# A decoder layer in split float32r: every weight product 256 columns wide, three in a row on one PSUM region

## The chip, the cores and the metric

The kernel runs on one core of one Trainium2 chip. The metric is device time in microseconds; the figure shown for the kernel before is the median of three runs. The profile is one execution, whose span runs from the first to the last instruction.

## What is computed

One layer of a hybrid decoder on a residual stream h of 256 rows by 2048, all float32: a half-step SwiGLU feed-forward network (FFN 1), token mixing, cross-attention to 256 memory rows, and a second half-step FFN (FFN 2). Cut to what the change touches:

```python
def swiglu_ffn(x, w_gu, w_down):                 # w_gu 2048 x 11264, w_down 5632 x 2048
    gate, up = jnp.split(x @ w_gu, 2, axis=-1)
    return (jax.nn.silu(gate) * up) @ w_down
...
    f = swiglu_ffn(rms_norm(h, ffn1_pre_g[l]), ffn1_w_gu[l], ffn1_w_down[l])
    h = h + FFN_RES_SCALE * rms_norm(f, ffn1_post_g[l])
    z = rms_norm(h, mix_pre_g[l]) @ w_in[l]      # conv a and g, then q, k, v, 1024 columns each
...
    y = jnp.concatenate([conv_out, attn], axis=-1) @ w_out[l]
    h = h + rms_norm(y, mix_post_g[l])
    c = memory_cross_attention(...)              # 4 heads of 128
    h = h + rms_norm(c, xattn_post_g[l])
    f = swiglu_ffn(rms_norm(h, ffn2_pre_g[l]), ffn2_w_gu[l], ffn2_w_down[l])
```

The two FFNs hold most of the arithmetic. The convolution group has a depthwise convolution with 31 taps, which is worked off on VectorE and on ScalarE with GpSimd.

## The kernel before

**Three products for one.** Each float32 operand is split into two float32r parts: `hi`, a copy of it rounded by ScalarE, and `lo`, what is left of it after VectorE has subtracted `hi`. A product x w is then taken as x_hi w_hi + x_lo w_hi + x_hi w_lo, three matmuls that accumulate in PSUM. The rows of x lie transposed in chunks (`ck` in the profile), where `xk[:, 0, :]` is the high and `xk[:, 1, :]` the low part of the 256 tokens for one k, a block of 128 rows of the contraction; the two lie next to each other, so that `xk` is also an operand of 512 columns.

**Weights.** Class `Weights` lists all weight tiles (128 x 1024, 512 KB) in the order of their use. SyncE loads them into `raw` (4 buffers), ScalarE makes `hi` (4 buffers, lines 177 and 179), VectorE `lo` (3 buffers, lines 193 and 195). A few tiles that are used later than they are split are held in chunks. Between tiles, class `Background` issues other work: gates, norms, convolution taps, attention.

**Four ways of multiplying.**
- `proj_T` (lines 423 and 426): the weights are stationary, the rows move, 256 columns wide. For a k and its regions (a region is half a PSUM bank, 256 columns) it issues first the two products with `hi`, region after region, then all products with `lo`. It is used for the first two of the 22 groups of gate and up in each FFN, for the GLU of the convolution group, for q and k, for the memory's keys (`kv_k`) and for the queries of the cross-attention.
- `gate_up` for the other 20 groups (lines 637 and 639): the weights are stationary and `xk` moves as one operand of 512 columns, into four banks in turn, so that a bank's left half gets x_hi w_hi and its right half x_lo w_hi; then four products of `lo` with x_hi, 256 wide, go on top of the right halves. A group thus holds four banks, and each has two partial sums.
- `proj` (lines 434, 436, 438): the rows are stationary and the weights move, 512 columns wide, over one or two banks in turn. It is used by `down` (FFN down and the output projection), for v, and for the output of the cross-attention. In `down` the last three tiles of the second half are kept back and go region by region, nine products on one bank.
- The values of the cross-attention (`mm_xv`, lines 1078 to 1080): rows stationary, weights moving, 256 columns wide, the three products of one region in a row. The change leaves this one as it is.

**The gate.** `queue_gate` lays the work on a finished group into the background: `add_parts` copies the right halves out of PSUM on ScalarE and adds the left halves on VectorE (for the first two groups it only copies), then come the scale, the SiLU, the product of gate and up, and its split into `hi` and `lo`.

Of the kernel before, what the change touches and what calls it, by code (L numbers as in the profile page):

```python
# [14 lines left out]
P = 128  # L15
# [27 lines left out]
class Background:  # L43
    """Work that is issued a piece at a time between the weight tiles."""
# [13 lines left out]
    def urgent(self, pieces):  # L58
        """Each of the pieces in a step of its own, before all else that waits."""
        for fn, dve, act in reversed(pieces):  # L60
            self.main.appendleft(None)
            self.main.appendleft((fn, dve, act, 0.0))
# [33 lines left out]
class Weights:  # L96
    """The weights in the order of their use: loads, then the two float32r parts, ahead of the products."""
# [22 lines left out]
    def start(self):  # L120
        """The first rows and weights, in halves."""
# [24 lines left out]
    def parts(self, i, whole):  # L146
        """The pieces of an entry that have a gain each: (raw, part of the tile, gain)."""
# [76 lines left out]
def layer_kernel(ctx: ExitStack, tc: tile.TileContext, x, mem, eye, consts, smalls, post_g, xt, memt,  # L224
# [127 lines left out]
    class Rows:  # L352
        """Transposed float32r parts of [256, 2048] rows, and their 1 / rms."""
# [64 lines left out]
    def proj_T(regions, first, last, hi, lo, xk, parts_first=False):  # L418
        order = [(f, r) for f in range(2) for r in enumerate(regions)]
        if not parts_first:  # L420
            order = [(f, r) for r in enumerate(regions) for f in range(2)]
        for f, (j, (ps, o)) in order:
            nc.tensor.matmul(ps[:, o:o + 256], hi[:, j * P:(j + 1) * P], xk[:, f, :],  # L423
                             start=first and o == 0 and f == 0, stop=False, skip_group_check=True)
        for j, (ps, o) in enumerate(regions):
            nc.tensor.matmul(ps[:, o:o + 256], lo[:, j * P:(j + 1) * P], xk[:, 0, :],  # L426
                             start=False, stop=last, skip_group_check=True)

    def proj(pss, first, last, hi, lo, xk, t, n0=0):
        xh = xk[:, 0, t * P:(t + 1) * P]  # L430
        xl = xk[:, 1, t * P:(t + 1) * P]
        cols = [slice((n0 + n) * 512, (n0 + n + 1) * 512) for n in range(len(pss))]
        for ps, c in zip(pss, cols):
            nc.tensor.matmul(ps, xh, hi[:, c], start=first, stop=False)  # L434
        for ps, c in zip(pss, cols):
            nc.tensor.matmul(ps, xl, hi[:, c], start=False, stop=False)  # L436
        for ps, c in zip(pss, cols):
# [820 lines left out]
```

## Time and profile before

| | us |
|---|---|
| median of 3 runs (1978.13 to 1981.71) | 1979.76 |
| span of the profiled execution | 1979.2 |
| TensorE busy | 1925.5 (97%) |
| VectorE busy | 1268.0 (64%) |
| ScalarE busy | 1098.7 (56%) |
| GpSimd busy | 204.8 (10%) |

In the profile a matmul has two parts, the load of its stationary operand (LDWEIGHTS, listed as PEld) and the product itself (MATMUL, listed as PE); 11034 of each ran. Matmuls are pipelined, so that the durations of neighbours overlap, and how fast a stream goes is read from the distance between starts. FFN 1's gate and up run from the start to 500 us, its down phase to 745 us, token mixing to 1137 us, cross-attention to 1234 us, FFN 2's gate and up to 1724 us, its down phase to the end. The granted TensorE clock is 0.997 of 2.4 GHz over the span.

### The profile page before, as it was taken

What the parts mean: (1) busy time and instruction counts of PE and PEld (TensorE: products, weight loads), DVE (VectorE), ACT (ScalarE), POOL (GpSimd) and SP (SyncE); (2) the same over time, 40 slices, a digit from 0 to 9 for tenths busy, and PEclk for the clock granted to TensorE, in tenths of its full rate; (3) what the DMA queues carried; (4) which work ended last, traced back from release to release, by engine and by line L of the source; (5) the groups of instructions that cost most, each with busy time, mean ns of one, the idle gap of its engine ahead of it and who ended that gap; (6) DMA issues with size and microseconds to landing.
All of it is one profiled execution on the core that took longest, in us unless ns stands there. A gap on an engine that the chain in (4) does not pass through costs nothing.

```text
span 1979.2 us, 29214 instructions
## 1 busy us (share of the span) xinstructions
PE 1925.5 (97%) x11034; PEld 1675.8 (85%) x11034; DVE 1268.0 (64%) x1774; ACT 1098.7 (56%) x1793; POOL 204.8 (10%) x192
## 2 busy tenths in 40 slices
PE   8999999999999999887899999999999999999998
PEld 8888888888888889886797898988888888888886
DVE  5666666666544556999767576666666666644444
ACT  6655555555434646766465565755555555533433
POOL 0000000000000000768401000000000000000000
PEclk9999999999999999999999999999999999999999
DMA  8666666666655774344555653566666666666664
GB/s 289 187 190 191 191 192 190 189 189 192 210 191 187 256 244 141 130 149 139 166 165 169 214 179 120 181 191 191 188 189 191 191 191 192 212 188 187 189 189 142
DMA packets 102094, 369.62 MB, mean 187 GB/s; under 512 B 11456, under 2 KB 11712, under 8 KB 101184
## 3 DMA queue, kind: packets, MB, share of 16 engines
q1 hardware_dynamic: 100944, 361.00, 58.5%
q10 hardware_dynamic: 1008, 6.75, 0.9%
q8 instruction: 86, 1.41, 0.3%
q14 instruction: 56, 0.46, 0.1%
HBM read 365.61 MB, written 2.10 MB: 186 GB/s over the span
## 4 chain that ended last, share of the span: by engine, by line
PE 89%; DVE 6%; issue 2%; POOL 2%; ACT 1%; DMA 1%; SPq 0%; DVEq 0%; POOLq 0%; ACTq 0%
PE ps L637 30%; PE ps L639 15%; PE ps L438 11%; PE ps L434 10%; PE ps L436 10%; PE ps L423 7%; PE ps L426 3%; DVE lo L195 3%; DVE cv L747 2%; POOL cv L758 1%; PE ps L339 0%; DMA raw<-in_f_gu_dram 0%; ACT hi L179 0%; PE ps L1080 0%; PE ps L1078 0%
## 5 line engine op out<-in xcount | busy, mean ns | idle before, releaser
L195 DVE SCALAR_TENSOR_TENSOR lo<-raw,sm,hi 128x512 fp32r<-128x512 f32 (+1 forms) x830 | 636.4, 806 | 335.1 <-issue 249.3
L179 ACT ACTIVATE hi<-raw,sm 128x512 fp32r<-128x512 f32 (+1 forms) x830 | 576.4, 741 | 374.8 <-PE ps L637 220.9
L637 PE MATMUL ps<-ck,hi 128*128 128x512 f32 x2560 | 693.4, 393 | 0.0
L637 PEld LDWEIGHTS ps<-ck,hi 128*128 128x128 f32 x2560 | 434.5, 188 | 55.0
L193 DVE TENSOR_TENSOR lo<-raw,hi 128x1024 fp32r<-128x1024 f32 x216 | 265.4, 1230 | 282.4 <-PE ps L438 248.6
L639 PEld LDWEIGHTS ps<-ck,lo 128*128 128x128 f32 x2560 | 388.0, 188 | 53.8
L639 PE MATMUL ps<-ck,lo 128*128 128x256 f32 x2560 | 399.5, 278 | 0.0
L177 ACT ACTIVATE hi<-raw 128x1024 fp32r<-128x1024 f32 x216 | 228.7, 1060 | 297.2 <-PE ps L436 253.0
L438 PE MATMUL ps<-lo,ck 128*128 128x512 f32 x896 | 286.6, 397 | 9.1 <-DVE lo L195 7.8
L434 PE MATMUL ps<-hi,ck 128*128 128x512 f32 x896 | 286.7, 397 | 1.0 <-ACT ck L347 1.0
L436 PE MATMUL ps<-hi,ck 128*128 128x512 f32 x896 | 285.2, 396 | 0.0
L423 PE MATMUL ps<-ck,hi 128*128 128x256 f32 x1664 | 229.3, 283 | 9.5 <-ACT hi L140 6.2
L423 PEld LDWEIGHTS ps<-ck,hi 128*128 128x128 f32 x1664 | 210.2, 189 | 10.6 <-ACT hi L140 6.2
L438 PEld LDWEIGHTS ps<-lo,ck 128*128 128x128 f32 x896 | 168.1, 188 | 53.5 <-DVE lo L195 10.9
L436 PEld LDWEIGHTS ps<-hi,ck 128*128 128x128 f32 x896 | 168.3, 188 | 41.8 <-DVE ck L350 0.4
L434 PEld LDWEIGHTS ps<-hi,ck 128*128 128x128 f32 x896 | 168.0, 188 | 41.6 <-ACT ck L347 1.2
L606 POOL TENSOR_TENSOR tmp<-tmp,rb 128x512 f32<-128x512 f32 x44 | 58.2, 1322 | 1125.1 <-ACT tmp L605 1105.8
L426 PE MATMUL ps<-ck,lo 128*128 128x256 f32 x832 | 129.4, 283 | 23.3 <-DVE lo L195 23.3
L426 PEld LDWEIGHTS ps<-ck,lo 128*128 128x128 f32 x832 | 110.5, 188 | 28.3 <-DVE lo L195 28.2
L758 POOL TENSOR_TENSOR cv<-cv,cf 128x255 f32<-128x255 f32 (+14 forms) x120 | 106.3, 887 | 31.9 <-ACT cf L757 23.7
L747 DVE SCALAR_TENSOR_TENSOR cv<-yv,cf,cv 128x255 f32<-128x255 f32 (+14 forms) x120 | 85.1, 709 | 2.7
L598 DVE TENSOR_TENSOR tmp<-ps,tmp 128x256 f32<-128x256 f32 x160 | 60.1, 417 | 10.2 <-ACT tmp L597 10.2
(142 smaller groups left out, 925.8 us busy)
## 6 DMA issues: line engine op xcount, KB each, us to landing
raw<-in_f_gu_dram SPq DMA_DIRECT2D x351, 512.0 KB, 4.1
raw<-in_f_down_dram SPq DMA_DIRECT2D x176, 512.0 KB, 4.3
raw<-in_w_in_dram SPq DMA_DIRECT2D x80, 512.0 KB, 3.6
raw<-in_w_out_dram SPq DMA_DIRECT2D x32, 512.0 KB, 3.6
cf<-in_post_g_dram ACTq DMA_DIRECT2D x4, 1024.0 KB, 6.9
raw<-in_x_k_dram SPq DMA_DIRECT2D x8, 512.0 KB, 3.9
raw<-in_x_q_dram SPq DMA_DIRECT2D x8, 512.0 KB, 4.3
raw<-in_x_o_dram SPq DMA_DIRECT2D x8, 512.0 KB, 4.3
```

The source lines that it names most:

```text
L177: self.nc.scalar.activation(dst, src, AF.Copy)
L179: self.nc.scalar.activation(dst, src, AF.Copy, scale=g)
L193: self.nc.vector.tensor_tensor(dst, src, hi.bitcast(F32), ALU.subtract)
L195: self.nc.vector.scalar_tensor_tensor(dst, src, g, hi.bitcast(F32), ALU.mult, ALU.subtract)
L423: nc.tensor.matmul(ps[:, o:o + 256], hi[:, j * P:(j + 1) * P], xk[:, f, :], start=first and o == 0 and f == 0, stop=False, skip_group_chec ...
L426: nc.tensor.matmul(ps[:, o:o + 256], lo[:, j * P:(j + 1) * P], xk[:, 0, :], start=False, stop=last, skip_group_check=True)
L434: nc.tensor.matmul(ps, xh, hi[:, c], start=first, stop=False)
L436: nc.tensor.matmul(ps, xl, hi[:, c], start=False, stop=False)
L438: nc.tensor.matmul(ps, xh, lo[:, c], start=False, stop=last)
L637: nc.tensor.matmul(ps, hi[:, w], xk, start=k == 0, stop=False, skip_group_check=True)
L639: nc.tensor.matmul(ps[:, 256:512], lo[:, w], xk[:, 0, :], start=False, stop=k == KT - 1, skip_group_check=True)
L758: nc.gpsimd.tensor_tensor(cv[:, ct, s:], cv[:, ct, s:], pr[:, :S - s], ALU.add)
```

## The change

- `proj_T` issues for each region its three products in a row: `hi` with x_hi, `hi` with x_lo, `lo` with x_hi. Only the very first k of an FFN's first group keeps the three parts apart.
- `proj` takes each 512 columns in two halves of 256, and for each half the three products in a row.
- `gate_up` uses `proj_T` for all 22 groups, with two banks to a group. There are no partial sums any more, and `add_parts` is gone: the scale and the product of gate and up read PSUM themselves.

All weights, loads and splits stay, and so do the buffers. The comments and docstrings that the diff removes are left out here.

```diff
     def proj_T(regions, first, last, hi, lo, xk, parts_first=False):
-        order = [(f, r) for f in range(2) for r in enumerate(regions)]
-        if not parts_first:
-            order = [(f, r) for r in enumerate(regions) for f in range(2)]
-        for f, (j, (ps, o)) in order:
-            nc.tensor.matmul(ps[:, o:o + 256], hi[:, j * P:(j + 1) * P], xk[:, f, :],
-                             start=first and o == 0 and f == 0, stop=False, skip_group_check=True)
-        for j, (ps, o) in enumerate(regions):
-            nc.tensor.matmul(ps[:, o:o + 256], lo[:, j * P:(j + 1) * P], xk[:, 0, :],
-                             start=False, stop=last, skip_group_check=True)
+        order = [(r, i) for r in enumerate(regions) for i in range(3)]
+        if parts_first:
+            order = [(r, i) for i in range(3) for r in enumerate(regions)]
+        for (j, (ps, o)), i in order:
+            nc.tensor.matmul(ps[:, o:o + 256], (hi, hi, lo)[i][:, j * P:(j + 1) * P], xk[:, i % 2, :],
+                             start=first and o == 0 and i == 0, stop=last and i == 2, skip_group_check=True)
 
     def proj(pss, first, last, hi, lo, xk, t, n0=0):
-        xh = xk[:, 0, t * P:(t + 1) * P]
-        xl = xk[:, 1, t * P:(t + 1) * P]
-        cols = [slice((n0 + n) * 512, (n0 + n + 1) * 512) for n in range(len(pss))]
-        for ps, c in zip(pss, cols):
-            nc.tensor.matmul(ps, xh, hi[:, c], start=first, stop=False)
-        for ps, c in zip(pss, cols):
-            nc.tensor.matmul(ps, xl, hi[:, c], start=False, stop=False)
-        for ps, c in zip(pss, cols):
-            nc.tensor.matmul(ps, xh, lo[:, c], start=False, stop=last)
+        xs = [xk[:, f, t * P:(t + 1) * P] for f in (0, 1, 0)]
+        for n, ps in enumerate(pss):
+            for o in (0, 256):
+                c = slice((n0 + n) * 512 + o, (n0 + n) * 512 + o + 256)
+                for i, w in enumerate((hi, hi, lo)):
+                    nc.tensor.matmul(ps[:, o:o + 256], xs[i], w[:, c], start=first and o == 0 and i == 0,
+                                     stop=last and i == 2, skip_group_check=True)
...
     def queue_gate(G, U, rows, hi_, lo_):
         box = []
 
-        def add_parts(pss):
-            s = tmp()
-            box.append(s)
-            if len(pss) == 1:
-                nc.scalar.copy(s, pss[0])
-                return
-            for i, ps in enumerate(pss):
-                c = slice(i * 256, (i + 1) * 256)
-                nc.scalar.copy(s[:, c], ps[:, 256:512])
-                nc.vector.tensor_tensor(s[:, c], ps[:, 0:256], s[:, c], ALU.add)
-
         def gate():
-            add_parts(G)
-            nc.vector.tensor_tensor(two(box[0]), two(box[0]), bc2(rows.rb), ALU.mult)
+            box.append(tmp())
+            nc.vector.tensor_tensor(two(box[0]), two(G), bc2(rows.rb), ALU.mult)
...
         def product():
-            nc.vector.tensor_tensor(box[0], box[0], box[1], ALU.mult)
+            nc.vector.tensor_tensor(box[0], box[0], U, ALU.mult)
             make_hi(hi_, two(box[0]))
 
-        bg.add(gate, dve=1.3, act=0.8)
+        bg.add(gate, dve=0.7)
         bg.cut()
         bg.add(silu, act=0.5, pool=1.2)
-        bg.add(lambda: add_parts(U), dve=0.7, act=0.8)
         bg.cut()
...
         for g in range(2 * NG):
-            few = g < 2
-            pss = [bank() for _ in range(2 if few else 4)]
+            pss = [bank() for _ in range(2)]
 
             def mm(u, hi, lo):
                 for e in range(2):
                     k = 2 * u + e
-                    xk = rows.x(k)
-                    if few:
-                        proj_T(regions_of(pss), k == 0, k == KT - 1, hi[:, e * 512:], lo[:, e * 512:], xk, g == k == 0)
-                        continue
-                    ws = [slice(e * 512 + j * P, e * 512 + (j + 1) * P) for j in range(4)]
-                    for ps, w in zip(pss, ws):
-                        nc.tensor.matmul(ps, hi[:, w], xk, start=k == 0, stop=False, skip_group_check=True)
-                    for ps, w in zip(pss, ws):
-                        nc.tensor.matmul(ps[:, 256:512], lo[:, w], xk[:, 0, :], start=False, stop=k == KT - 1,
-                                         skip_group_check=True)
+                    proj_T(regions_of(pss), k == 0, k == KT - 1, hi[:, e * 512:], lo[:, e * 512:], rows.x(k),
+                           g == k == 0)
```

How the order moves, at three places. The names are the tile written (`ps_700` is a PSUM bank) and the tiles read, the moving operand first; sizes are those of the output.

TensorE, FFN 1, one k of a gate/up group before:

```order
L637 MATMUL ps_700<-ck_150,hi_758 128x512
L637 MATMUL ps_701<-ck_150,hi_758 128x512
L637 MATMUL ps_702<-ck_150,hi_758 128x512
L637 MATMUL ps_703<-ck_150,hi_758 128x512
L639 MATMUL ps_700<-ck_150,lo_786 128x256
L639 MATMUL ps_701<-ck_150,lo_786 128x256
L639 MATMUL ps_702<-ck_150,lo_786 128x256
L639 MATMUL ps_703<-ck_150,lo_786 128x256
```

TensorE, a k of the changed kernel with the same rows (`x2` stands for two products in a row on one region; a bank's name comes twice, once for each half):

```order
L424 MATMUL ps_699<-ck_150,hi_735 128x256 x2
L424 MATMUL ps_699<-ck_150,lo_772 128x256
L424 MATMUL ps_699<-ck_150,hi_735 128x256 x2
L424 MATMUL ps_699<-ck_150,lo_772 128x256
L424 MATMUL ps_700<-ck_150,hi_735 128x256 x2
L424 MATMUL ps_700<-ck_150,lo_772 128x256
```

The 512-wide products are gone, the `lo` products stand between those of `hi`, and two banks do for a group.

TensorE, the down phase of FFN 1 before, one tile and one half of the tokens:

```order
L434 MATMUL ps_4950<-hi_5096,ck_1338 128x512
L434 MATMUL ps_4951<-hi_5096,ck_1338 128x512
L436 MATMUL ps_4950<-hi_5096,ck_1338 128x512
L436 MATMUL ps_4951<-hi_5096,ck_1338 128x512
L438 MATMUL ps_4950<-lo_5116,ck_1338 128x512
L438 MATMUL ps_4951<-lo_5116,ck_1338 128x512
```

and in the changed kernel, the same piece of another tile:

```order
L434 MATMUL ps_6013<-hi_6264,ck_1500 128x256 x2
L434 MATMUL ps_6013<-lo_6296,ck_1500 128x256
L434 MATMUL ps_6013<-hi_6264,ck_1500 128x256 x2
L434 MATMUL ps_6013<-lo_6296,ck_1500 128x256
L434 MATMUL ps_6014<-hi_6264,ck_1500 128x256 x2
```

Six products of 512 columns that alternate between two banks have become twelve of 256, three in a row on a half bank (the last seven of them are like the five rows shown).

VectorE, FFN 1's gate and up before, one group's gate among the `lo` parts of the weights:

```order
L195 SCALAR_TENSOR_TENSOR lo<-raw,sm,hi 128x512 x10
L598 TENSOR_TENSOR tmp<-ps,tmp 128x256 x2
L602 TENSOR_TENSOR tmp<-tmp,rb 128x512
L195 SCALAR_TENSOR_TENSOR lo<-raw,sm,hi 128x512 x2
L598 TENSOR_TENSOR tmp<-ps,tmp 128x256 x2
L195 SCALAR_TENSOR_TENSOR lo<-raw,sm,hi 128x512 x2
L609 TENSOR_TENSOR tmp<-tmp 128x512
L195 SCALAR_TENSOR_TENSOR lo<-raw,sm,hi 128x512 x2
L350 TENSOR_TENSOR ck<-tmp,ck 128x2x256
```

and in the changed kernel:

```order
L195 SCALAR_TENSOR_TENSOR lo<-raw,sm,hi 128x512 x10
L587 TENSOR_TENSOR tmp<-ps,rb 128x512
L195 SCALAR_TENSOR_TENSOR lo<-raw,sm,hi 128x512 x4
L594 TENSOR_TENSOR tmp<-tmp,ps 128x512
L195 SCALAR_TENSOR_TENSOR lo<-raw,sm,hi 128x512 x2
L350 TENSOR_TENSOR ck<-tmp,ck 128x2x256
```

The additions of line 598 are gone, and the two others read the bank; a group has 18 `lo` pieces around them, before and now.

## Rows read from the trace of the kernel before

**Rows 1.** The page, chain that ended last, share of the span by line.

```profile
PE ps L637 30%; PE ps L639 15%; PE ps L438 11%; PE ps L434 10%; PE ps L436 10%; PE ps L423 7%; PE ps L426 3%; DVE lo L195 3%; DVE cv L747 2%; POOL cv L758 1%; PE ps L339 0%; DMA raw<-in_f_gu_dram 0%; ACT hi L179 0%; PE ps L1080 0%; PE ps L1078 0%
```

**Rows 2.** By stretches: length, busy PE, PEld, DVE, ACT, POOL, clock, DMA share, GB/s.

```profile
57.00:499.60 442.60, 442.60 (x2562) 388.20 (x2561) 291.01 (x456) 258.08 (x440) 27.93 (x21) 1.00 0.64 191
785.00:870.00 85.00, 72.07 (x588) 69.64 (x588) 81.53 (x106) 61.75 (x119) 59.86 (x69) 1.00 0.44 140
928.00:986.00 58.00, 50.14 (x195) 38.20 (x194) 48.56 (x52) 27.34 (x34) 30.38 (x21) 0.94 0.51 161
```

**Rows 3.** TensorE in order of time, gate/up: start us, us, line, tiles, count.

```profile
112.22 1.09 PE L637 MATMUL ps<-ck,hi 128*128 128x512 f32 x4
113.15 0.62 PE L639 MATMUL ps<-ck,lo 128*128 128x256 f32 x4
113.61 1.07 PE L637 MATMUL ps<-ck,hi 128*128 128x512 f32 x4
114.52 0.63 PE L639 MATMUL ps<-ck,lo 128*128 128x256 f32 x4
114.99 1.09 PE L637 MATMUL ps<-ck,hi 128*128 128x512 f32 x4
```

**Rows 4.** TensorE in order of time, the down phase of FFN 1.

```profile
540.16 0.63 PE L434 MATMUL ps<-hi,ck 128*128 128x512 f32 x2
...
551.36 0.63 PE L434 MATMUL ps<-hi,ck 128*128 128x512 f32 x2
```

**Rows 5.** TensorE in order of time, first group of FFN 1, by `proj_T`.

```profile
28.18 1.10 PE L423 MATMUL ps<-ck,hi 128*128 128x256 f32 x8
29.12 0.63 PE L426 MATMUL ps<-ck,lo 128*128 128x256 f32 x4
29.59 1.10 PE L423 MATMUL ps<-ck,hi 128*128 128x256 f32 x8
...
45.13 1.10 PE L423 MATMUL ps<-ck,hi 128*128 128x256 f32 x8
```

**Rows 6.** TensorE in order of time, the values of the cross-attention.

```profile
1180.18 0.28 PE L1080 MATMUL ps<-lo,ck 128*128 128x256 f32 x1
...
1182.22 0.28 PE L1080 MATMUL ps<-lo,ck 128*128 128x256 f32 x1
...
1186.91 0.28 PE L1079 MATMUL ps<-hi,ck 128*128 128x256 f32 x1
1187.03 0.28 PE L1080 MATMUL ps<-lo,ck 128*128 128x256 f32 x1
1187.15 0.28 PE L1078 MATMUL ps<-hi,ck 128*128 128x256 f32 x1
```

**Rows 7.** TensorE in order of time, last tiles of FFN 1's down phase.

```profile
737.99 0.39 PE L434 MATMUL ps<-hi,ck 128*128 128x512 f32 x1
...
739.86 0.39 PE L438 MATMUL ps<-lo,ck 128*128 128x512 f32 x1
```

**Rows 8.** TensorE in order of time, output of the cross-attention, weights held in chunks.

```profile
1218.35 0.39 PE L434 MATMUL ps<-ck 128*128 128x512 f32 x1
...
1224.47 0.39 PE L434 MATMUL ps<-ck 128*128 128x512 f32 x1
```

**Rows 9.** Waits of TensorE: us in total, times, longest us.

```profile
PE ps L426 <- DVE lo L195: 23.3, 24, 1.5
PE ps L438 <- DVE lo L195: 7.8, 6, 3.1
```

**Rows 10.** TensorE in order of time, GLU group, after a wait.

```profile
811.13 1.07 PE L423 MATMUL ps<-ck,hi 128*128 128x256 f32 x8
...
812.49 1.07 PE L423 MATMUL ps<-ck,hi 128*128 128x256 f32 x8
```

**Rows 11.** The page, costliest groups: count, busy us, mean ns, idle before and releaser.

```profile
L637 PE MATMUL ps<-ck,hi 128*128 128x512 f32 x2560 | 693.4, 393 | 0.0
L598 DVE TENSOR_TENSOR tmp<-ps,tmp 128x256 f32<-128x256 f32 x160 | 60.1, 417 | 10.2 <-ACT tmp L597 10.2
```

More of the change, by code (lines that the diff above doesn't have):

```diff
@@ L646, in gate_up @@
             c = slice(2 * (g % 2), 2 * (g % 2) + 2)
-            queue_gate(pss[:len(pss) // 2], pss[len(pss) // 2:], rows, hT[-1][:, c, 0, :], hT[-1][:, c, 1, :])
+            queue_gate(pss[0], pss[1], rows, hT[-1][:, c, 0, :], hT[-1][:, c, 1, :])
         return hT
```

## The prediction

> **What bounds the kernel now.** I read the chain of waits first: five of its six largest entries are matmul lines, 30, 15, 11, 10 and 10% of the span [rows 1]. So I asked next where TensorE has no gaps. In the table by stretches FFN 1's gate/up phase shows TensorE busy for all of its 442.6 us and VectorE for 291 (FFN 2 issues the same stream); in the convolution stretch VectorE is busy for 81.5 of 85 us and TensorE for only 72.1 [rows 2]. So the two gate/up phases and the two down phases go at TensorE's pace, and the stretch from 785 to 956 us goes at that of VectorE's taps and `lo` parts; the list of waits says the same, 23.3 us in 24 waits of L426 on `lo` and 7.8 us in 6 of L438 [rows 9].
>
> What is to be priced is therefore the distance from one product's start to the next, not its duration (matmuls overlap, and their ends are modelled). I read it from starts in the order of time, as (last start - first start) / products between:
> - gate/up now, for one k: four 512-wide and four 256-wide products. Two k take 114.99 - 112.22 = 2.77 us [rows 3]; over a whole phase 442.6 us / 320 = 1.383 us for one k [rows 2].
> - down now, 512 wide, the weights moving: 48 products in 551.36 - 540.16 = 11.20 us, 233.3 ns each [rows 4].
> - `proj_T` now, 256 wide, the rows moving and the weights stationary: 144 products in 45.13 - 28.18 = 16.95 us, 117.7 ns each [rows 5].
> - the cross-attention's values (L1078 to L1080), 256 wide, the weights moving, three products of one region in a row: 18 in 1182.22 - 1180.18 = 2.04 us, 113.3 ns each [rows 6].
>
> The last is the form that the change gives to everything. Two things in it are new to the other lines: the width and the order. Which of the two makes it fast decides the sign, so I looked for rows that separate them.
>
> **Does the order matter?** Three rows say no. In the 256-wide `proj_T` the first eight products of a k come in pairs on a region and the last four change region each time: 29.12 - 28.18 = 0.94 us for eight and 29.59 - 29.12 = 0.47 us for four, 117.5 ns in either [rows 5]. In gate/up the four `lo` products go to four different banks, and take 113.61 - 113.15 = 0.46 and 114.99 - 114.52 = 0.47 us, 115 to 118 ns each, no more than those of `proj_T` [rows 3]. And at the end of the down phase nine 512-wide products stand in a row on one region, and still take (739.86 - 737.99) / 8 = 234 ns [rows 7], what they take when they alternate [rows 4]. So keeping a region for three products buys nothing by itself.
>
> **Does the pace depend on what moves, and from where?** It seems so. 512 columns of weights from the `hi` and `lo` buffers take 233.3 ns [rows 4], from the held chunks 6.12 us / 27 = 226.7 ns [rows 8], and 256 columns from `hi` and `lo` 113.3 ns [rows 6]. After a break the values' stream starts slower and settles at 113.3 within a few products: the first two steps read 0.12 us each [rows 6]. `proj_T` has two paces: after one wait on `lo` a k took 812.49 - 811.13 = 1.36 us, 113.3 ns for each product, until the next wait [rows 10]; but the steady pace where nothing waits is 117.7 [rows 5]. I take the quicker one for a phase relation that a break can set by chance and that long streams do not enter.
>
> **The change, part by part.**
>
> 1. Gate and up, 20 groups of 16 k in each FFN: 640 k. Twelve 256-wide `proj_T` products replace four of 512 and four of 256; columns are the same (3,072), instructions are half as many again. At 117.7 ns a k takes 1.412 us instead of 1.383: +0.029 x 640 = **+19 us**. At 113.3 ns it would take 1.360: -0.023 x 640 = -15 us. Those are the bounds; I take the upper, since the operands' roles and places are those of rows 5 and only the order differs.
>
> 2. Down, both FFNs: 2 x 88 tiles x 12 = 2,112 products of 512 become pairs of 256 in the very form of rows 6. 2 x 113.3 - 233.3 = -6.7 ns each: **-14.1 us**. If 256 columns cost 117.7 here too, +2.1 ns each, +4 us.
>
> 3. The output projection (384 products) and v (192) likewise: -2.6 us, and of v's -1.3 us about half, since VectorE sets the pace of the first half of that stretch (TensorE 50.1 of 58 us [rows 2]): together **-3.2 us**. The held output weights of the cross-attention run at 226.7 for 512 already [rows 8] and give nothing.
>
> 4. `proj_T` elsewhere (the first two groups of each FFN, GLU, q/k, cross-attention q): order only. By the argument above **0**; -7.6 us (some 1,700 products outside the waits, 4.4 ns each) if the order matters.
>
> 5. The first `lo` product is now third in its k instead of ninth (or of 17th in the q/k groups, fifth in v). Where TensorE waits for `lo` at every tile, VectorE sets the pace and the time of a tile stays; but when that stretch ends, TensorE has some six products more to do behind the last wait, 6 x 117.7 ns = 0.7 us, and about half of that after the first weights' arrival at the start. **+1.1 us**, between 0 and +3.
>
> 6. The partial sums: 160 ACT copies and 160 VectorE additions go (417 ns each, 60.1 us on VectorE [rows 11]). All of that lies beside 442 us of unbroken matmuls [rows 2]; it ends nothing: **0**. It frees two of the four banks of a group, and no product of L637 ever waited for one (idle 0.0 [rows 11]): 0.
>
> Sum: 19 - 14.1 - 3.2 + 1.1 = +2.8 us on the profiled span of 1979.2, 1982.0; the median of the runs is 0.6 above that span, so **1982.6 us**, taken as 1982.5.
>
> The Trainium skill speaks against the change: its page "TensorE: Matmul & The Clock Gate", section "Back-to-back issue gap", gives N/2.4 + 2.5 ns for each product, so that two of 256 would cost 2.5 ns more than one of 512. By that the 2,560 + 2,688 split products would add an estimated 13 us. The trace does not follow it: 512 took 233.3 or 226.7 ns here and 256 took 117.7 or 113.3.
>
> **The rivals.**
>
> *The order matters after all.* Then every `proj_T` goes at 113.3 ns: -15 - 7.6 - 14.1 - 3.2 + 1.1 = -38.8, **1941 us**. For it: the one place that has this order is fast every time, and the quick stretch of rows 10 shows that `proj_T` can go so. Against it: rows 3, 5 and 7. A half of it, one of the two gate/up phases falling into that quick pace by chance, gives 1982.5 - 17 = 1965.
>
> *Narrow products are dearer everywhere.* A slowdown by one mechanism: each 256-wide product in down costs what it costs in `proj_T`, 117.7 ns, so that the pair is 2.1 ns above the one of 512. Items 2 and 3 turn from -17.3 into +5.6: **2005 us**. It decides from 116.7 ns per product on. For it: `proj_T`, the larger part of today's 256-wide products, runs so wherever nothing disturbs it [rows 5]; against it: rows 6 have down's roles and buffers exactly. The page named above would put the same sign on it.
>
> *The earlier `lo` stalls TensorE.* If in the convolution stretch VectorE's `lo` waited in turn for buffers that TensorE now gives back later, each of the 30 waits [rows 9] would grow by 0.7 us, +21: **2003 us**. Against it: TensorE idles before each of those waits, so that buffers come back before VectorE needs them.
>
> **How the numbers follow.** The forecast, with its own range 1979 to 1989, has 0.50; order matters 0.25; half of that 0.08; narrow is dearer 0.11; stalls 0.06. What a measurement of this kernel can tell from no change is about 0.2%, 4 us: 1975.8 to 1983.7. Of the forecast's 0.50 I put 0.30 within it and 0.20 above, since the small open terms are all costs. Faster: 0.25 + 0.08 = 0.33; same 0.30; slower 0.20 + 0.11 + 0.06 = 0.37. The range reaches down to the order rival and up past the forecast's own, 1938 to 1990, and leaves out the two slow rivals, 0.17.
>
> **What the profile after would show.** Gate/up: 12 products at 117.7 ns, 452 us a phase; at 435 us the order (or that phase relation) made it. Down: pairs at 226.7 ns, its two halves some 7 us shorter in each FFN; at 235 the narrow rival. Waits of the third product on `lo` between 805 and 956 us, as many as now, of about 0.7 us more each with the stretch no longer. The wrong step would most likely be the claim that the order is nothing: it rests on other widths and roles than those it is used for.

## The result and the profile after

The changed kernel took **1996.34 us** in the median of five executions (1988.34 to 2002.73) against 1979.76 before: ratio 1.0075, 95% interval 1.005 to 1.0101: slower, by less than 1% but clear of the noise. The forecast was 1982.5, its range ended at 1990. The profiled execution of the changed kernel was one of the shorter ones, 1988.62 us with a span of 1986.8, so the profile alone can show only part of the gap.

Its page, the chain that ended last (answers to [rows 1]), the waits of TensorE ([rows 9]) and four groups by line (count, busy us, mean ns, idle before):

```profile
PE ps L424 54%; PE ps L434 31%; DVE lo L195 3%; DVE cv L722 2%; POOL cv L733 1%; DMA raw<-in_f_gu_dram 1%; PE ps L339 0%; ACT hi L179 0%; PE ps L1055 0%; PE ps L1053 0%; PE ps L1054 0%; DMA raw<-in_x_v_dram 0%; DVE lo L193 0%; DVE h L477 0%
```

```profile
PE ps L424 <- DVE lo L195: 25.9, 26, 2.0
PE ps L434 <- DVE lo L195: 7.0, 5, 3.2
```

```profile
L424 PE MATMUL ps<-ck,hi 128*128 128x256 f32 x6784 | 1204.7, 280 | 7.8 <-ACT hi L140 6.8
L424 PE MATMUL ps<-ck,lo 128*128 128x256 f32 x3392 | 949.3, 280 | 25.9 <-DVE lo L195 25.9
L434 PE MATMUL ps<-hi,ck 128*128 128x256 f32 x3584 | 617.6, 278 | 1.3 <-ACT ck L347 1.0
L434 PE MATMUL ps<-lo,ck 128*128 128x256 f32 x1792 | 497.9, 278 | 9.5 <-DVE lo L195 7.0
```

The bound is what it was: matmul lines make 85% of the chain, and the waits on `lo` are 31 now, 32.9 us together, where 30 made 31.1. The mean durations of 278 and 280 ns say nothing about the pace, because neighbours overlap. Starts do. One view serves for the rest of this document, the table by stretches; its columns are the stretch and its length, then busy us and (x instructions) of PE, PEld, DVE, ACT and POOL, the clock, the DMA share and GB/s. The four stretches lie inside FFN 1's gate/up, FFN 1's down, FFN 2's gate/up and FFN 2's down. The changed kernel:

```profile
100.00:500.00 400.00, 400.00 (x3398) 400.00 (x3398) 234.42 (x338) 208.86 (x319) 23.33 (x18) 1.00 0.56 187
520.00:660.00 140.00, 140.00 (x1238) 140.00 (x1237) 66.05 (x56) 56.53 (x59) 0.00 (x0) 1.00 0.61 205
1300.00:1700.00 400.00, 400.00 (x3398) 400.00 (x3398) 233.08 (x335) 208.66 (x319) 23.35 (x18) 1.00 0.57 187
1760.00:1930.00 170.00, 170.00 (x1503) 170.00 (x1502) 79.17 (x67) 69.17 (x71) 0.00 (x0) 1.00 0.61 194
```

Length by count is the distance from one product to the next: 400/3398 = 117.7 ns in both gate/up phases and 140/1238 = 113.1, 170/1503 = 113.1 in both down phases. (Each count has two or three products that began before the stretch; from starts the values are 117.78 and 113.33.) In order of time, [rows 4] have this answer:

```profile
539.95 0.39 PE L434 MATMUL ps<-hi,ck 128*128 128x256 f32 x2
540.17 0.28 PE L434 MATMUL ps<-lo,ck 128*128 128x256 f32 x1
...
542.33 0.39 PE L434 MATMUL ps<-hi,ck 128*128 128x256 f32 x2
```

21 products lie between the first and the last row: 2.38 us / 21 = 113.3 ns. The one place that went the other way from the rest is the output of the cross-attention, [rows 8]; 192 products of 256 in

```profile
1210.73 23.38 PE L434 MATMUL ps<-ck 128*128 128x256 f32 x192
```

are 121 ns apart on average and 120 in most steps, where 512 columns took 226.7.

The two traces against each other, start of the first product of each part:

| starts at | before | after | shift | longer (+) or shorter (-) since the row above |
|---|---|---|---|---|
| FFN 1's third group | 53.86 | 53.71 | -0.15 | |
| FFN 1 down | 499.56 | 508.99 | +9.43 | +9.58 |
| first product after it | 746.39 | 750.14 | +3.75 | -5.68 |
| GLU | 781.58 | 785.57 | +3.98 | +0.2 |
| v | 927.21 | 932.81 | +5.60 | +1.6 |
| attention | 986.48 | 990.78 | +4.30 | -1.3 |
| output projection | 1039.58 | 1043.79 | +4.21 | -0.1 |
| cross-attention | 1137.86 | 1141.25 | +3.39 | -0.8 |
| its output | 1207.25 | 1210.73 | +3.48 | +0.1 |
| FFN 2 | 1234.25 | 1239.02 | +4.78 | +1.3 |
| FFN 2 down | 1724.25 | 1738.55 | +14.29 | +9.5 |
| last product | 1970.42 | 1978.12 | +7.69 | -6.6 |

So this execution is 7.7 us longer inside the span: 19 lost in gate and up, 12.3 won back in down, 1.0 lost between. The median lies another 7.7 us above it. Where that went, only the experiments told.

### The profile page after: what moved, and what is told of

Read it like the earlier page. It is cut to its first block, busy times and chain, and to the rows that moved or that the text cites. A ratio compares the mean times of both kernels' runs of the same rounds, so it can differ in the third digit from the quotient of the medians.

```text
span 1986.8 us, 39665 instructions
## 1 busy us (share of the span) xinstructions
PE 1931.2 (97%) x16378; PEld 1919.3 (97%) x16378; DVE 1215.7 (61%) x1614; ACT 1054.2 (53%) x1625; POOL 204.2 (10%) x192
## 4 chain that ended last, share of the span: by engine, by line
PE 88%; DVE 6%; issue 2%; POOL 2%; ACT 1%; DMA 1%; SPq 0%; DVEq 0%; POOLq 0%; ACTq 0%
PE ps L424 54%; PE ps L434 31%; DVE lo L195 3%; DVE cv L722 2%; POOL cv L733 1%; DMA raw<-in_f_gu_dram 1%; PE ps L339 0%; ACT hi L179 0%; PE ps L1055 0%; PE ps L1053 0%; PE ps L1054 0%; DMA raw<-in_x_v_dram 0%; DVE lo L193 0%; DVE h L477 0%; DMA raw<-in_xt_dram 0%
## 5 line engine op out<-in xcount | busy, mean ns | idle before, releaser
L424 PE MATMUL ps<-ck,hi 128*128 128x256 f32 x6784 | 1204.7, 280 | 7.8 <-ACT hi L140 6.8
L424 PEld LDWEIGHTS ps<-ck,hi 128*128 128x128 f32 x6784 | 1037.1, 188 | 9.1 <-ACT hi L140 6.8
L424 PE MATMUL ps<-ck,lo 128*128 128x256 f32 x3392 | 949.3, 280 | 25.9 <-DVE lo L195 25.9
L424 PEld LDWEIGHTS ps<-ck,lo 128*128 128x128 f32 x3392 | 635.2, 187 | 31.2 <-DVE lo L195 31.2
L434 PE MATMUL ps<-hi,ck 128*128 128x256 f32 x3584 | 617.6, 278 | 1.3 <-ACT ck L347 1.0
L434 PEld LDWEIGHTS ps<-hi,ck 128*128 128x128 f32 x3584 | 543.2, 189 | 2.2 <-ACT ck L347 1.2
L434 PE MATMUL ps<-lo,ck 128*128 128x256 f32 x1792 | 497.9, 278 | 9.5 <-DVE lo L195 7.0
L434 PEld LDWEIGHTS ps<-lo,ck 128*128 128x128 f32 x1792 | 338.0, 189 | 11.4 <-DVE lo L195 8.4
L732 ACT ACTIVATE cf<-yv,cf 128x255 f32<-128x255 f32 (+14 forms) x120 | 54.7, 487 | 16.3 <-POOL cv L733 15.7
L347 ACT ACTIVATE ck<-tmp 128x512 fp32r<-128x512 f32 x44 | 27.8, 633 | 42.3 <-DVE tmp L594 42.3
```

The lines of the kernel that those rows point to most:

```text
L347: nc.scalar.activation(hi, src, AF.Copy)
L424: nc.tensor.matmul(ps[:, o:o + 256], (hi, hi, lo)[i][:, j * P:(j + 1) * P], xk[:, i % 2, :], start=first and o == 0 and i == 0, stop=last ...
L434: nc.tensor.matmul(ps[:, o:o + 256], xs[i], w[:, c], start=first and o == 0 and i == 0, stop=last and i == 2, skip_group_check=True)
L732: nc.scalar.activation(pr[:, :S - s], yv[:, ct, :S - s], AF.Copy, scale=w)
```

## The experiments

**1. One half of the change at a time.** The first kernel has the new `proj` and everything else as before; the second has the new `proj_T` and `gate_up`, and the old `proj`.

```diff
 # e1_down_only: the changed kernel with the old proj_T, gate_up and add_parts
 # e2_gu_only: the changed kernel with
-        xs = [xk[:, f, t * P:(t + 1) * P] for f in (0, 1, 0)]
-        for n, ps in enumerate(pss):
-            for o in (0, 256):
...
+        for ps, c in zip(pss, cols):
+            nc.tensor.matmul(ps, xh, hi[:, c], start=first, stop=False)
...
```

> Only proj takes 256 columns, three products of a region in a row; gate_up and proj_T as before. Theory (a 256-wide stream with moving weights has two paces, 113.3 and 117.8 ns, and an execution settles at one of them by chance): gate/up stays at 1.383 us for a k; the two down phases take either 240 us (113.3) or 250 us (117.8) each, against 246.5 before, so the time lies between 1966 and 1987 us and spreads by several us from run to run. Rival (the pace of down was as forecast in every run, and the loss sits elsewhere, in gate/up or in the waits): all runs at 1964 to 1968 us with little spread.

> Only gate_up, proj_T and the gate change; proj keeps its 512 columns. Theory: gate/up at 117.8 ns for a product, 452 us a phase, +19 us, so 1997 to 2001 us, and runs that agree within 3 us, since the stream whose pace varies is not in this kernel. Rival (the two paces can be taken by any 256-wide stream, gate/up too): runs that spread over 10 us and more, some of them near 1965 (gate/up at 113.3).

Measured: `e1_down_only` 1967.06 us (1965.75 to 1969.14), ratio 0.9934 [0.992, 0.9949]; `e2_gu_only` 1998.95 (1996.87 to 2000.28), 1.0094 [1.0079, 1.0109]. Against 1980.49 for the kernel before on that chip these are -13.4 and +18.5 us. One stretch of gate/up and one of down, first of the kernel before, then of `e1_down_only`, then of `e2_gu_only`:

```profile
100.00:500.00 400.00, 400.00 (x2314) 350.85 (x2313) 261.44 (x414) 230.57 (x394) 23.45 (x18) 1.00 0.63 191
520.00:660.00 140.00, 140.00 (x602) 112.20 (x601) 63.62 (x55) 56.62 (x63) 0.00 (x0) 1.00 0.63 202
```

```profile
100.00:500.00 400.00, 400.00 (x2318) 350.96 (x2317) 262.08 (x413) 231.10 (x395) 23.50 (x18) 1.00 0.59 192
520.00:660.00 140.00, 140.00 (x1238) 140.00 (x1237) 64.88 (x56) 59.25 (x69) 0.00 (x0) 1.00 0.66 207
```

```profile
100.00:500.00 400.00, 400.00 (x3398) 400.00 (x3398) 234.57 (x338) 209.09 (x320) 23.40 (x18) 1.00 0.57 187
520.00:660.00 140.00, 140.00 (x602) 112.20 (x601) 63.65 (x54) 55.45 (x58) 0.00 (x0) 1.00 0.59 194
```

The half of the change that is not in a kernel keeps its old pace, the other half has the new one. The two effects add up to +5.1 us; the traced executions of the whole change with both down phases quick lie 6 to 9 us above before, so that within a few us the effects do not touch each other. The long executions of the whole change are not in that sum. Down alone is the better kernel, faster than either of the two compared. I had expected its times to spread over both paces, up to 1987 us; they lie within 3.4 us, as the rival had it. By these times none of its eight down phases was slow (two of them are traced, at 113.3 ns). Eight are too few to say whether the slow start needs the new gate/up ahead of it.

**2. The order.** The changed kernel with the old order in `proj_T` (both `hi` products of each region, then all `lo`), the width kept.

```diff
-        order = [(r, i) for r in enumerate(regions) for i in range(3)]
...
+            order = [(f, r) for r in enumerate(regions) for f in range(2)]
```

> The changed kernel with the old order inside proj_T: per region two products with hi, then all products with lo; still 256 wide and without partial sums. Theory (order is nothing): gate/up again at 117.8 ns and 452 us a phase; time as that of the changed kernel, 1988 to 2003. Rival (three in a row is what costs, for instance by the earlier lo): gate/up or the waits shorter, at least 5 us less than the changed kernel.

Measured: 1992.98 us (1986.83 to 1996.36), 1.007 [1.0052, 1.0088], as the changed kernel; both gate/up phases at 117.78 ns, both down phases at 113.3. The order in `proj_T` buys and costs nothing; the order in `proj` was not undone by itself.

**3. The place of the rows.** If the order is nothing, why do equal widths go at 113.3 and 117.7? What is left is which operand is stationary, and where the operands lie. A filler of 64, 128 or 256 bytes for each partition ahead of the chunks moves all rows against all weights (and the other tiles of that pool with them).

```diff
+    shift = ap.tile([P, 16], F32, name="shift")      # 64 bytes; 32 and 64 elements in the others
+    nc.gpsimd.memset(shift, 0.0)
```

> The changed kernel with 64 bytes of padding ahead of the tiles of pool ap, so that the chunks of the rows lie 64 bytes later against the hi and lo buffers. Theory (where the two operands lie sets the pace): gate/up and down go at other paces than 117.8 and 113.3 ns, by 2 ns or more in one of them, 10 us or more in the time. Rival (width and role alone set it): both paces as in the changed kernel, 117.8 and 113.3 or 117.8.

> The changed kernel with 128 bytes of padding ahead of the row chunks. Theory (the pace goes by stationary minus moving address modulo 256: 64 gives 113.3, 192 gives 117.8, 128 some 118.7, 0 gives 120): the two roles change places; gate/up at 113.3 ns, 435 us a phase, down at 117.8, 250 us a phase; about 1966 to 1976 us. Rival (each shift away from the tuned place only costs): both at 117 ns or more, above 1995 us.

> The changed kernel with 256 bytes of padding. Theory (modulo 256): nothing changes, gate/up 117.8 and down 113.3 ns. Rival (modulo 512 or more): other paces.

> The same padding under the kernel that has the change in gate_up and proj_T alone; proj takes 512 columns as before. Theory: gate/up at 113.3 ns, 435 us a phase, the 512-wide down at most the 233.3 ns of the kernel before: 1952 to 1962 us. Rival: gate/up at 117.8, 452 us a phase, 1997 us or more.

Measured: with 64 bytes 2023.71 us (2022.48 to 2027.23), 1.0222 [1.0207, 1.0238]; with 128 bytes 1978.46 (1954.81 to 1984.99), 0.9935 [0.9896, 0.9974]; with 256 bytes 1985.59, one execution, as without a filler; with 128 bytes and the old `proj` 1968.21 (1952.22 to 1973.0), 0.9919 [0.9884, 0.9953]. (With 128 bytes the times lie in groups, so that the median and the ratio say different things.) First one gate/up and one down stretch with 64 bytes, then all four with 128:

```profile
100.00:500.00 400.00, 400.00 (x3374) 400.00 (x3373) 232.30 (x335) 209.31 (x318) 23.14 (x18) 1.00 0.56 186
520.00:660.00 140.00, 140.00 (x1182) 140.00 (x1181) 63.52 (x55) 55.07 (x58) 0.00 (x0) 1.00 0.57 185
```

```profile
100.00:500.00 400.00, 400.00 (x3399) 400.00 (x3398) 234.19 (x337) 208.99 (x319) 23.28 (x18) 1.00 0.56 187
520.00:660.00 140.00, 140.00 (x1192) 140.00 (x1191) 62.80 (x54) 54.43 (x58) 0.00 (x0) 1.00 0.59 191
1300.00:1700.00 400.00, 400.00 (x3532) 400.00 (x3531) 245.38 (x351) 216.39 (x332) 23.31 (x19) 1.00 0.60 194
1760.00:1930.00 170.00, 170.00 (x1502) 170.00 (x1501) 78.95 (x67) 68.47 (x71) 0.00 (x0) 1.00 0.57 194
```

With 64 bytes both phases go at 118.7 ns from start to start, down included. With 128 the same code goes at two paces in one execution: 117.7 ns in FFN 1's gate/up and 117.5 in its down, 113.3 and 113.2 in FFN 2's. In FFN 1 and in FFN 2 down begins at the pace that gate/up had, and stays at it. I had expected the two roles to change places; half of that came, gate/up at 113.3 in FFN 2 and down at 117.5 in FFN 1. So the place matters, with a period of 256 bytes as far as tried, but it doesn't settle the pace: here is a second choice that an execution makes. The spread of the times says so too: ten executions with 128 bytes fall into two groups, 1955 to 1958 and 1978 to 1985; seven with the old `proj` into 1952 and 1968 to 1973.

**4. Can gate/up be pushed to the quick pace?** A guess from 3: a stream carries on the pace of the stream ahead of it. So 24 additional products ahead of the third group of each FFN, into a spare bank that nobody reads: in `e5_settle` with the rows stationary, down's form; in `e6_control` with the weights stationary, as in `proj_T`.

```diff
+                    if g == 2 and k == 0:
+                        spare, xk = bank(), rows.x(0)
+                        for i in range(24):
+                            nc.tensor.matmul(spare[:, 0:256], xk[:, (0, 1, 0)[i % 3], 0:P],
+                                             (hi, hi, lo)[i % 3][:, 0:256], start=i == 0, stop=i == 23)
```

> The changed kernel, with 24 extra products into a spare bank at the start of each FFN's third gate/up group, in the form that settles at 113.3 ns (weights move, rows are stationary). Theory (the pace is a relation between neighbouring products that is carried on until something breaks it): the proj_T stream behind them goes on at 113.3 ns, 435 us for a gate/up phase instead of 452, twice, for 2 x 2.7 us of extra products: 1954 to 1960 us in most runs, 30 us less than the changed kernel. Rival (place and role alone fix the pace): gate/up at 117.8, some 1992 us.

> The same 24 extra products, but in the form of proj_T (rows move, weights are stationary). Both theories: gate/up stays at 117.8 ns, 452 us a phase; the time is that of the changed kernel and 2 x 2.8 us, 1990 to 2003 us. If it too falls to 435 us a phase, it was the pause or the spare bank and not the form that set the pace.

> The changed kernel once more, unaltered, for the spread of its times (1988 to 2003 in five runs) and a second trace. If the profiled execution is one of the long ones, theory one (the pace of a stream settles differently from run to run) shows a gate/up or down phase at another pace than 117.8 and 113.3 ns; theory two (transfers or engines stall TensorE now and then) shows the same paces and more time in waits.

Measured: `e5_settle` 1983.33 us (1975.61 to 1991.54), 1.0021 [1.0008, 1.0035]; `e6_control` 1996.96 (1991.7 to 2001.46), 1.0094 [1.0075, 1.0113]; the changed kernel again 1986.91 (1978.69 to 1995.78), 1.0032 [1.0017, 1.0047]. The traces of all three have gate/up at 117.78 ns, and the 24 products of `e5_settle` themselves went at 117 to 118: they did not settle, so there was nothing to carry, and the guess was not put to the test in that execution. It took 1989.94 us, one of the three longest; the nine others took 1975.61 to 1983.69 and have no trace. Whether a gate/up phase went at the quick pace in those stays open.

**5. Does a break decide the pace of a down phase?** In the two traces that the changed kernel had by then the first steps of down, from start to start, were about 118, 123, 118, 114 and 113 ns, and it was quick from there. One plain float32 product ahead of the first down product breaks the stream; it goes into a spare bank.

```diff
             def mm(k, hi, lo):
+                if hf == 0 and k == 0 and nk == KF:      # e8_break_ffn2: keep in place of nk == KF, FFN 2 alone
+                    spare = bank()
+                    nc.tensor.matmul(spare[:, 0:P], ones, ones, start=True, stop=True)
```

> The changed kernel with one plain float32 product (ones times ones into a spare bank) ahead of each FFN's first down product, so that the stream is broken there. Theory (down settles at 113.3 from the stream before it, and a break can leave it at 117.8 for good): in the trace one or both down phases at 117.8 ns, 250 instead of 240 us, +9 or +19 us. Rival (moving weights pull every stream to 113.3 at this placement): both down phases at 240 us, time as that of the changed kernel, 1987.

> The changed kernel unaltered, for a trace of one more execution. Its times fall into groups near 1987, 1996 to 1998 and 2002. If this execution is one of the longer ones: theory one (a down phase at 117.8 ns, +9.4 us) shows 250 us for a down phase; theory two (a gate/up phase at 120 ns, +8.5 us) shows 461 us for a gate/up phase; theory three (waits) shows neither. If it is near 1987: 452 and 240 us, as in the two traces so far.

Measured: `e7_break` **2005.82** us (2005.12 to 2006.57), 1.0134 [1.0117, 1.0151]; the changed kernel beside it 1986.02, its two down phases at 113.3 ns. In order of time, then the down stretches of FFN 1 and FFN 2:

```profile
509.31 0.38 PE L489 MATMUL ps<-ones 128*128 128x128 f32 x2
509.45 0.48 PE L434 MATMUL ps<-hi,ck 128*128 128x256 f32 x2
509.76 0.28 PE L434 MATMUL ps<-lo,ck 128*128 128x256 f32 x1
509.88 0.40 PE L434 MATMUL ps<-hi,ck 128*128 128x256 f32 x2
510.12 0.28 PE L434 MATMUL ps<-lo,ck 128*128 128x256 f32 x1
```

```profile
520.00:660.00 140.00, 140.00 (x1191) 140.00 (x1190) 62.95 (x55) 54.93 (x58) 0.00 (x0) 1.00 0.57 189
1760.00:1930.00 170.00, 170.00 (x1446) 170.00 (x1445) 76.10 (x65) 66.06 (x68) 0.00 (x0) 1.00 0.57 186
```

The product itself delays the stream by some 0.2 us. But what follows goes at 117.8 ns from start to start, and 1191 products in 140 us (without the extra product 1238) show that it lasts. The phases took 249.1 and 248.7 us instead of 240.0 and 239.6 in the changed kernel's trace of experiment 4: two short breaks cost 19 us. The rival, that moving weights pull every stream to 113.3 at this placement, falls. The spare bank also shifts the banks of the products behind it; but by the built programs FFN 1's down phase begins in the same four banks in `e5_settle` and `e6_control`, where it went at 113.3, so that the banks are not the reason.

**6. The long executions.** If the pace of a down phase is chosen at its start, the changed kernel may choose otherwise by itself: at some 9 us a phase there would be executions near 1987, 1996 and 2005 us. One kernel has the break in FFN 2 alone; three are the changed kernel, unaltered.

> The changed kernel with the one plain float32 product ahead of FFN 2's first down product alone (it goes into a bank that nobody reads); FFN 1 as in the changed kernel. With it ahead of both down phases the time was 2005.8 us and both phases went at 117.8 ns for a product. Theory (a phase keeps the pace that its start gives it): FFN 2's down phase at 117.8 ns, 248.7 us, FFN 1's at 113.3, about 240; the time half way, 1987 + 9.2 = 1996 us, where the long executions of the changed kernel lie. Rival (the loss with two products came from something that only both bring): nearer 1987 or 2006.

> The changed kernel unchanged. Of its executions so far most lie near 1987 us and some at 1996 to 2003, and no trace is of a long one. If this one is long, theory: one of its four FFN phases goes at another of the paces seen (a down phase at 117.8 ns instead of 113.3, +9.2 us, or a gate/up phase at 120 instead of 117.8, +8.6), the rest unchanged. Rival: all stretches are longer by the same share, 0.5%. If it is short, at 1985 to 1989 us, the phases are at 117.8 ns (gate/up) and 113.3 (down).

> As the other: the changed kernel unchanged. If this execution is long, theory: one of its four FFN phases at another of the paces seen (a down phase at 117.8 ns instead of 113.3, +9.2 us, or a gate/up phase at 120 instead of 117.8, +8.6). Rival: all stretches longer by the same share, 0.5%. If short, 1985 to 1989 us with 117.8 ns and 113.3.

> As the two others: the changed kernel unchanged. If this execution is long, theory: one of its four FFN phases at another of the paces seen (a down phase at 117.8 ns instead of 113.3, +9.2 us, or a gate/up phase at 120 instead of 117.8, +8.6). Rival: all stretches longer by the same share, 0.5%. If short, 1985 to 1989 us with 117.8 ns and 113.3.

Measured: `e8_break_ffn2` 2000.62 us, ratio 1.011 [1.0083, 1.0138], in two pairs, 1996.03 and 1996.17, 2005.07 and 2005.74; the changed kernel 1986.6, 1993.12 and 1995.58 us. In the traced execution of `e8_break_ffn2`, 1996.17 us, FFN 2's down phase is slow (248.7 us) and FFN 1's quick, as expected:

```profile
520.00:660.00 140.00, 140.00 (x1238) 140.00 (x1237) 65.01 (x56) 55.99 (x59) 0.00 (x0) 1.00 0.63 205
1760.00:1930.00 170.00, 170.00 (x1446) 170.00 (x1445) 76.35 (x65) 66.42 (x69) 0.00 (x0) 1.00 0.57 187
```

Its other pair is 9 us longer, which would be FFN 1's down phase slow of itself; that pair has no trace. Of the changed kernel the last two are the long executions that were missing. The two down stretches of the one of 1993.12, then of that of 1995.58:

```profile
520.00:660.00 140.00, 140.00 (x1238) 140.00 (x1237) 65.99 (x56) 56.29 (x59) 0.00 (x0) 1.00 0.63 206
1760.00:1930.00 170.00, 170.00 (x1445) 170.00 (x1445) 76.30 (x65) 66.46 (x69) 0.00 (x0) 1.00 0.57 187
```

```profile
520.00:660.00 140.00, 140.00 (x1191) 140.00 (x1190) 63.47 (x54) 55.42 (x58) 0.00 (x0) 1.00 0.58 190
1760.00:1930.00 170.00, 170.00 (x1502) 170.00 (x1502) 79.05 (x67) 68.58 (x71) 0.00 (x0) 1.00 0.58 194
```

In the first FFN 2's down phase is slow (248.4 us from first to last product), in the second FFN 1's (249.1), and the other one is quick (240.1 and 239.6). Gate/up is at 117.7 in both, as in every trace at this placement; the rival, all stretches longer by one share, falls. The start of FFN 1's down phase, first in the execution of 1986.6 us, then in that of 1995.58:

```profile
508.04 0.28 PE L424 MATMUL ps<-ck,lo 128*128 128x256 f32 x1
508.15 0.40 PE L434 MATMUL ps<-hi,ck 128*128 128x256 f32 x2
508.39 0.28 PE L434 MATMUL ps<-lo,ck 128*128 128x256 f32 x1
508.51 0.39 PE L434 MATMUL ps<-hi,ck 128*128 128x256 f32 x2
508.73 0.28 PE L434 MATMUL ps<-lo,ck 128*128 128x256 f32 x1
```

```profile
508.79 0.28 PE L424 MATMUL ps<-ck,lo 128*128 128x256 f32 x1
508.90 0.40 PE L434 MATMUL ps<-hi,ck 128*128 128x256 f32 x2
509.13 0.28 PE L434 MATMUL ps<-lo,ck 128*128 128x256 f32 x1
509.25 0.40 PE L434 MATMUL ps<-hi,ck 128*128 128x256 f32 x2
509.49 0.28 PE L434 MATMUL ps<-lo,ck 128*128 128x256 f32 x1
```

No engine waits at either place. The steps between starts, the first being that from the last `proj_T` product, are 118, 123, 118, 114, 113 ns in the one and 115, 117, 117, 118, 118 in the other. From its fourth step on the first is 4 ns quicker with each product; the second never gets there. What gives the first step its 118 or 115 is open; the code and its order are the same.

A break alone does not decide it. Half-way through FFN 1's down phase two other float32 products (line 389) interrupt the stream in every trace; here in the changed kernel's first trace, then in that of 1995.58 us:

```profile
677.65 0.59 PE L389 MATMUL ps<-tmp,ones 128*128 128x256 f32 x2
677.89 0.59 PE L434 MATMUL ps<-hi,ck 128*128 128x256 f32 x2
```

```profile
684.15 0.59 PE L389 MATMUL ps<-tmp,ones 128*128 128x256 f32 x2
684.40 0.59 PE L434 MATMUL ps<-hi,ck 128*128 128x256 f32 x2
```

Behind them the quick phase goes on with steps of 122, 116, 114 and 113 ns, the slow one with 118 throughout: each takes its own pace up again. And a quick phase can fall: in each quick FFN 2 phase of the changed kernel one step of some 170 ns near the end is followed by 57 products at 117.8.

All executions of the unaltered changed kernel, 19 from several chips, sort so: 13 up to 1988.62 us, five from 1993.12 to 1997.94, one at 2002.73. Six of them have a trace, four of the first group (no slow down phase) and two of the second (one); that the untraced ones follow the same rule is inferred from their times, and the one at 2002.73 is 2.4 us shorter than any execution with both breaks. Their median is 1988.14, 0.4% above before; the five that made the result were two, two and one from the three groups, and their median fell into the second.

## Why the prediction was wrong

**Item 1, gate and up: right.** +19 us was forecast, 9.58 + 9.5 = 19.1 measured, and +18.5 for that half alone. The choice of the upper bound, 117.7 ns, was the choice of [rows 5] over [rows 10], and every trace at this placement agrees. It holds for the placement alone: with 128 bytes gate/up went at 113.3 in three of four traced phases.

**Items 2 and 3, down and what shares its code: right in kind, 4 us too large.** -14.1 was forecast for the down phases, -5.7 and -6.6 measured. The output projection and v were to give -3.2; they gave -0.8 and -1.3, -2.1. Parts of the output projection go at the slower pace after a break: from 1044.7 to 1053.0 us, where nothing waits, its products are 117.8 ns apart. That the held output weights "give nothing" failed too: they cost 1.3 us, since two products of 120 ns took the place of one of 226.7. Its reason, that 512 columns were quick, was a reason for a loss.

**Items 4 to 6: right, as far as shown.** Order gave nothing (experiment 2). The earlier `lo` cost about what was put on it: the waits grew by 32.9 - 31.1 = 1.8 us, and the shift over the stretch of the GLU, q and k by 1.6, against a forecast of 1.1. The partial sums took 52 us from VectorE (1215.7 busy after 1268.0); that this is worth nothing was not tried by itself, but TensorE is busy for all 400 us of each gate/up stretch.

**The base: 1.2 us off.** I added 0.6 us for what lies outside the span, a median less the span of another execution. In the changed kernel's profiled execution, time and span belong together: 1988.62 - 1986.83 = 1.79. The sum for an execution with both down phases quick would then be 1983.8, where such executions took 1986 to 1989. (One small misreading: of the six largest entries of [rows 1] all are matmul lines, not five. Nothing hangs on it.)

**What broke it: item 2 has one pace for down.** It took 113.3 ns for all products of both phases in every execution, from 18 products of another stream [rows 6], which starts slower and "settles at 113.3 within a few products". That `proj_T` had two paces was in the rows, but was set aside: "I take the quicker one for a phase relation that a break can set by chance and that long streams do not enter." Neither holds for every long stream. A down phase that starts at 117.8 does not settle in 2,112 products (248.4 us instead of 239.6), and gate/up with 128 bytes went at 113.3 through whole phases. Each slow down phase costs 9 us (experiments 5 and 6), and the prediction had no term for one: the -14.1 of item 2 were -12.3 with both phases quick, some -4 in the traces with one slow, and +5 with both (`e7_break`). On the quick executions, 1986 to 1989 us, one slow phase gives 1995 to 1998; the median of 1996.34 lies there, though it has no trace itself. Of the 13.7 us from 1982.6 to it some 4.9 lie in the other sizes above, 1.2 in the base, and 7.7 in what the median has above the traced quick execution.

The rival "narrow products are dearer everywhere" had the right price, 117.7 ns in down, but I made it a matter of all or nothing, a property of width; some phases go at it and most do not, 7 of 38 by the sorting above. One of two phases, halfway between forecast and rival, is 1994, and the range had to hold it.

The rival of the order would have needed one quick gate/up, and undoing the order changed no pace (experiment 2). The rival of the stalls did not happen: the waits grew by 1.8 us in all, not by 21.

The rule of the Trainium skill cited ahead ("TensorE: Matmul & The Clock Gate", "Back-to-back issue gap") is given there for an isolated product; I had put it on long streams. It had the sign of the result but not for its reason: by it down alone should have lost, and it gained 13.4 us.

## What to carry to other kernels

Where a trace shows two paces for products of one width, price both for each long phase, and expect executions to differ by whole phases. When times fall into groups, look for one phase at another pace before looking for noise, and get a trace from each group. Of a change with two halves that do not touch, run each alone: here the half that keeps 512 columns in gate/up and takes 256 in down is 0.66% faster than before, while both together are slower.

## What the runs showed of the hardware

- 256 columns of float32r took about 113.3, 117.8, 118.7 or 120 ns from start to start at a granted clock of 1.00, with no wait in between. Which of them are open to a stream depends on where its stationary operand lies against the moving one. By the addresses in the built program, stationary less moving modulo 256 bytes was 64 or 192 for the streams at 113.3 and 117.8, 128 for those at 118.7 (the filler of 64 bytes), and 0 for those at 120 (the output of the cross-attention, both operands in chunks). That last stream is moved as a whole by the fillers, and its steps stayed at 120 with each of them; so it is not the address by itself. That is four placements, not a law. The wide products differ too: 512 columns took 233.3 ns at 64, 228.9 at 192 (the old `proj` with 128 bytes) and 226.7 at 0.
- At 64 and 192 streams were seen at two paces; one that nothing interrupts kept the one that it took within its first steps, for 240 us or longer, and experiment 6 shows breaks behind which a stream took its pace up again or fell to the slower one. One float32 product of 0.2 us ahead of each down phase moved both to the slower one (experiment 5, one execution traced, the three others within 1.5 us of it); without it, in the 23 down phases traced at this placement, a first step of 115 ns went with the slow pace (two phases) and one of 116 to 118 with the quick (21).
- Open: what sets that first step; why a few executions (1978.69 of the changed kernel, 1975.61 to 1984 in `e5_settle`) were shorter than any trace accounts for; why 2002.73 is not nearer 2005; and whether a product could be put ahead of gate/up that makes it start quick. With a filler of 128 bytes and the old `proj` both gate/up phases did so in a traced execution of 1952.47 us, the shortest with a trace; by their times, five of the seven executions did not.
